# Hybrid decoder layer on one core: the sums of the second SwiGLU's down weights made by accumulating transfers that GpSimd issues, in place of adds on VectorE

## The chip, the core and the metric

One core of one Trainium2 chip runs the whole layer as one program. The core has a matrix engine (TensorE, PE in the profile), a vector engine (VectorE, DVE), an activation engine (ScalarE, ACT), a general engine (GpSimd, POOL), a queue processor that issues transfers (SyncE, SP), and 16 DMA engines that move data between HBM and the on-chip SBUF. The engines run side by side and each takes its instructions strictly in order; semaphores hold an instruction until what it needs is there. The metric is the time of the program on the device, in microseconds (us). A change of under 0.5% is about what a measurement of this kernel can't tell from none.

## The reference

The layer has three residual parts: a SwiGLU with half weight, a mixer with two kinds of attention, and a second SwiGLU with half weight.

```
h = swiglu(rms_norm(x, ff1_norm_pre), ...);   x = x + 0.5 * rms_norm(h, ff1_norm_post)
h = hybrid_mixer(rms_norm(x, mix_norm_pre));  x = x + rms_norm(h, mix_norm_post)
h = swiglu(rms_norm(x, ff2_norm_pre), ...);   x = x + 0.5 * rms_norm(h, ff2_norm_post)

def swiglu(h, w_gate, w_up, w_down):
    return (jax.nn.silu(h @ w_gate) * (h @ w_up)) @ w_down
```

There are 512 tokens of width 1024; the inner width of a SwiGLU is 2816. All is float32. The change concerns the last product of the second SwiGLU, `(...) @ w_down`.

## The kernel before, in words

**Precision.** A float32 product is made of three passes of TensorE: each operand is split into a high part (a copy rounded to the engine's fast format) and a low part (what is left), and high x high, high x low and low x high are added. A split costs one copy on ScalarE (sometimes on VectorE) for the high part and one subtraction on VectorE for the low part (`split`, lines 397 and 400 of the profile).

**Fewer products.** In the SwiGLUs a product of 2 x 2 blocks is made of seven block products instead of eight; for that some operands are sums of blocks. In the second SwiGLU's down product, 16 of the 22 row blocks of `w_down` go this way (`down_products`, `factor`, `down_product`), the other six, called plain pieces, the ordinary way (`down_piece`, `down_mm`). The seven products come in the order 1, 5, 6, 2, 7, 4, 3, with half of the first two plain pieces between 7 and 4. Each product takes its weights in four quarters q = 0 to 3, and each quarter is 12 matmuls of 512 columns. The tiles `ff2dw{m}{q}h` and `l` hold the high and low part of product m, quarter q.

**The sums.** With blocks B00, B01, B10 and B11 of the down weights, product 5 needs B00 + B01, product 6 that sum + B11, product 4 that + B10, and product 7 needs B01 + B11. Products 1, 2 and 3 take a block as it is. A running sum per quarter stands in the tile `ff2du{q}`. In the kernel before, every block comes from HBM into a tile `rawff2d...` by a transfer of 512 KB that SyncE issues (function `raw`, line 326 of the profile), and VectorE adds it (function `add`, line 594): four quarters for each of the products 5, 6, 7 and 4, so 16 adds.

**What sets the order.** All steps are written down as a graph (`Graph.op`), each with its engine, an estimated cost and the tiles it touches. `Graph.order` simulates the engines with those costs and lets each take, among the ready steps, the one with the highest level (longest way to the end, plus a number from the table `BIAS` for its kind). The result is a fixed list, and the program is emitted in that list's order. Tiles are slots of pools: 4 for `raw` tiles, 6 of kind `M` (the `ff2du` tiles stand there), 12 of kind `ring` (the split weights, two a quarter); a step waits until a slot is free.

**Around it.** Before the down products, the gate and up products (`product`, line 657) run, at the head of the program behind a norm: `n1{t}_xn` is the normed row block t, `n1{t}_t` its transpose on TensorE, and `xa1`, `xa2`, `xa4`, `xa8` the split transposes (two row blocks in each); `ff1q00w0` and the like are split gate (`ff1q00`) and up (`ff1q01`) weights.

Of the kernel before, what the change touches and what calls it, by code (L numbers as in the profile page):

```python
# [18 lines left out]
P = 128  # L19
# [34 lines left out]
    "ACT:fh>fdl": 2, "ACT:fh>fdl@ACT": -102.8, "ACT:fh>fhh": 18.2, "ACT:fh>fhh@DVE": -182, "ACT:fhr>fhh": -133.1,
    "ACT:fhr>fhh@ACT": -164.3, "ACT:fhr>fhh@DVE": 0.1, "ACT:fp_>fp_": 142.4, "ACT:fqu>fqw": 85.2,
    "ACT:fqv>fqw": 175.9, "ACT:fy>fdp": -30.4, "ACT:fy>o_ss": 22, "ACT:gr>gh": 1551.9, "ACT:htv>hTv": -9.6,
    "ACT:k__t>kT": 13.9, "ACT:ls>ls": 43.9, "ACT:n_nm>n_l": -61.2, "ACT:n_t>n_th": -21.2, "ACT:n_t>xa": -27.9,
    "ACT:n_t>xaf0": -166.3, "ACT:n_t>xc": 937.3, "ACT:n_t>xcf0": -5.8, "ACT:n_t>xcf1": -136.4,
# [9 lines left out]
    "ACT:xrv>Xv@ACT": 109.7, "ACT:z>o_ss": 7, "DVE:acc>oN": -12.4, "DVE:cd_t>kc": 14.2, "DVE:ck>kcT": -14.4,
    "DVE:cmask>cmb": -123.5, "DVE:cmask>gates": -28.4, "DVE:cmk>uk": -45.7, "DVE:cmv>uv": 35.2, "DVE:cv>vc": -35.9,
    "DVE:d>d_p": -19.3, "DVE:d_acc>o": 29.2, "DVE:d_r>d_p": 28.8, "DVE:d_t>d_th": 53.2, "DVE:dkt>dk": 5,  # L70
    "DVE:dl>d_r": -27.9, "DVE:dl>do_r": 19.2, "DVE:dmask>dmb": 14.2, "DVE:do_rr>o": 39.5, "DVE:do_t>oTd": -11,
    "DVE:fa>fh": 68.2, "DVE:fa>fhs": 89.7, "DVE:fb>fhs": -62.8, "DVE:fb>fp_": -55.6, "DVE:fc>fp_": -201.2,
    "DVE:fc__sg>fh": 23.8, "DVE:fd>fhs": 83.8, "DVE:fdp>fy": -4, "DVE:fdq>fy": 2.1, "DVE:fdr>fy": 3.8,
    "DVE:fh>fds": -7.5, "DVE:fh>fhl": 155.6, "DVE:fh>fhl@DVE": 9.3, "DVE:fh>fhl@POOL": 1.1, "DVE:fhr>fhl": 41.3,
    "DVE:fp_>fh": 50.6, "DVE:fp_>fp_": 4.3, "DVE:fqu>fqw": -345.7, "DVE:fqv>fqw": 43.8, "DVE:gates>nc_pc": 247,
    "DVE:gr>gh": 533.4, "DVE:gsub>gsub": 93.5, "DVE:htk>hTk": -0.9, "DVE:htv>hTv": 40.2, "DVE:k__t>kT": 53.3,
    "DVE:lamt>lp": -116.6, "DVE:lp>ls": 76.6, "DVE:n_cf>n_p@ACT": -63.4, "DVE:n_cf>n_p@DVE": -25.6,
# [9 lines left out]
    "DVE:xcf1>xcf1": -33, "DVE:xi>n_xn": 1575.3, "DVE:xj>n_xn": 161.1, "DVE:xm>n_xn": 62.1, "DVE:xrk>Xk@DVE": 51.4,  # L87
    "DVE:xrk>Xk@POOL": -0.9, "DVE:xrv>Xv": 53.6, "DVE:xrv>Xv@DVE": 124.3, "DVE:xrv>Xv@POOL": -18.4,
    "DVE:z>o_yg": 28.8, "PE:cd>kc": 18.3, "PE:d_p>o": 12.8, "PE:d_th>d_acc": -4, "PE:dkd>dk": -89.8,
    "PE:fqw>fa": -1.5, "PE:fqw>fb": 32.4, "PE:fqw>fc": 7923.9, "PE:fqw>fd": 39.8, "PE:gh>g_": 1645.8,  # L90
    "PE:k__dup>kT": -44, "PE:n_p>n_th": 266.8, "PE:n_th>acc": 854.1, "PE:n_xn>n_t": 60.2, "PE:n_xn>xb": -54.9,
# [1453 lines left out]
```

## Time and profile before

| | |
|---|---|
| time, median of 3 runs | 1007.09 us (1005.99 to 1009.65) |
| time of the profiled execution | 1006.28 us |
| its span, first to last instruction | 1004.5 us |
| TensorE busy | 991.2 us (99%) |
| VectorE busy | 831.7 us (83%) |
| ScalarE busy | 581.3 us (58%) |
| GpSimd busy | 34.5 us (3%) |
| read from HBM, written to HBM | 135.45 MB, 19.92 MB |

The profiled execution's time is 1.78 us over its span; that part lies outside the first and the last instruction. TensorE's busy time is modelled at the ends of its matmuls, so that a matmul that waits for its operand can still count as busy for a part of the wait; a wait shows best where the next start comes late. The granted TensorE clock averages 0.998 over the span.

### The profile page before, as it was taken

How to read it: one execution, taken by the hardware profiler on the slowest of the kernel's cores; microseconds unless marked ns; L12 is line 12 of the kernel's file. 1: busy time of each engine (PE TensorE's matmuls, PEld its weight loads, DVE VectorE, ACT ScalarE, POOL GpSimd, SP SyncE). 2: the span in 40 equal slices, each digit the busy share in tenths (PEclk: the TensorE clock that was granted, in tenths of full speed). 3: DMA queues.
4: the chain of work that ended last, by engine and by line, in shares of the span. 5: the costliest groups of instructions: out<-in, count | busy, mean ns of one | idle time of the engine just before them, and what ended most of it. 6: DMA issues, size and time to landing. Idle time of an engine off the chain costs nothing. (4 is left out here: it accounts for less than half of the span.)

```text
span 1004.5 us, 17263 instructions
## 1 busy us (share of the span) xinstructions
PE 991.2 (99%) x6552; PEld 901.5 (90%) x6552; DVE 831.7 (83%) x1564; ACT 581.3 (58%) x1141; POOL 34.5 (3%) x68
## 2 busy tenths in 40 slices
PE   8999999999999999999999999999999999999997
PEld 7999999999888889888888888899999999987776
DVE  7999989987565488578787799899989988999984
ACT  8645545555455365677777677776455554544442
POOL 1000000000000030000000001310000000000001
PEclk9999999999999999999999999999999999999999
DMA  9226514118999535840403052261335231386752
GB/s 319 80 86 177 178 43 156 56 43 279 367 354 370 186 122 186 324 168 1 168 1 141 28 191 87 81 230 64 128 104 168 70 101 43 105 278 225 237 203 84
DMA packets 98437, 156.49 MB, mean 156 GB/s; under 512 B 11185, under 2 KB 63665, under 8 KB 98354
## 3 DMA queue, kind: packets, MB, share of 16 engines
q1 hardware_dynamic: 98354, 155.40, 45.0%
q8 instruction: 51, 0.84, 0.3%
q14 instruction: 32, 0.26, 0.1%
HBM read 135.45 MB, written 19.92 MB: 155 GB/s over the span
## 5 line engine op out<-in xcount | busy, mean ns | idle before, releaser
L1195 ACT ACTIVATE n_p<-n_p,n_nm 128x128 f32<-128x128 f32 (+3 forms) x64 | 35.4, 556 | 9.3 <-DVE n_nm L1193 8.9
L346 DVE TENSOR_TENSOR pre<-pre 128x1024 fp32r<-128x1024 f32 x20 | 24.1, 1222 | 19.8 <-ACT pre L345 19.7
L345 ACT CAST pre<-pre 128x1024 fp32r<-128x1024 f32 x20 | 21.0, 1052 | 23.6 <-DMA pre<-w_in 14.4
L1193 DVE CUSTOM_DVE_ANT_0 n_p<-n,dmb 128x128 f32<-128x128 f32 (+3 forms) x64 | 28.3, 486 | 6.2 <-PE n L1183 5.8
L400 DVE TENSOR_TENSOR n_th<-n_t,n_th 128x512 fp32r<-128x512 f32 x40 | 25.8, 682 | 9.2 <-ACT n_th L397 9.1
L432 POOL TENSOR_SCALAR o_ms<-o_ss 128x1 f32<-128x1 f32 x12 | 4.2, 349 | 670.2 <-ACT junk L440 670.1
L397 ACT CAST n_th<-n_t 128x512 fp32r<-128x512 f32 x40 | 21.5, 594 | 9.7 <-PE n_t L1298 9.5
L684 ACT ACTIVATE ff2p<-ff2p 128x256 f32<-128x256 f32 x30 | 12.5, 417 | 17.2 <-DVE ff2p L696 17.1
L684 ACT ACTIVATE ff1p<-ff1p 128x256 f32<-128x256 f32 x30 | 12.5, 416 | 16.1 <-DVE ff1p L696 15.5
L696 DVE TENSOR_TENSOR ff1p<-ff1p,ff1b 128x512 f32<-128x512 f32 x30 | 20.3, 678 | 1.1 <-PE ff1b L657 1.0
L1298 PE MATMUL n_t<-ident,n_p 128*128 128x128 f32 x160 | 20.7, 272 | 0.0
L1298 PEld LDWEIGHTS n_t<-ident,n_p 128*128 128x128 f32 x160 | 18.6, 140 | 2.2
L1195 ACT ACTIVATE d_p<-d_p,d_nm 128x128 f32<-128x128 f32 (+3 forms) x32 | 17.8, 556 | 4.8 <-DVE d_nm L1193 4.8
L696 DVE TENSOR_TENSOR ff2p<-ff2p,ff2b 128x512 f32<-128x512 f32 x30 | 20.4, 679 | 0.2 <-PE ff2b L657 0.2
L1182 PE MATMUL n<-kT,qTn 128*128 128x128 f32 (+3 forms) x64 | 20.3, 334 | 0.0
L1183 PE MATMUL n<-kT,qTn 128*128 128x128 f32 (+3 forms) x64 | 19.6, 321 | 0.0
L440 ACT ACTIVATE junk<-ff2y 128x512 bf16<-128x512 f32 x8 | 4.8, 597 | 22.9 <-PE ff2y L761 22.9
L562 DVE TENSOR_TENSOR o_yg<-ff2y,g_ff_norm_post 128x512 f32<-128x512 f32 x8 | 5.5, 688 | 14.3 <-ACT junk L440 14.3
L391 PE MATMUL acc<-n_th,v 128*64 128x512 f32 x40 | 16.1, 402 | 0.0
L1193 DVE CUSTOM_DVE_ANT_0 d_p<-d,dmb 128x128 f32<-128x128 f32 (+3 forms) x32 | 14.9, 485 | 1.4 <-PE d L1183 1.0
L392 PE MATMUL acc<-n_th,v 128*128 128x512 f32 x40 | 15.7, 392 | 0.0
L463 PE MATMUL n_t<-ident,n_xn 128*128 128x128 f32 x96 | 13.7, 293 | 1.4 <-DVE n_xn L456 1.3
(1743 smaller groups left out, 3477.9 us busy)
## 6 DMA issues: line engine op xcount, KB each, us to landing
rawff2d<-ff_w_down SPq DMA_DIRECT2D x36, 512.0 KB, 4.9
...
```

Source lines behind the costliest of these rows:

```text
L345: op("ACT", act(n, 0.04), lambda: A.copy(hi(), raw()), r=[(k, 0)], w=[(k, 1)])
L346: op("DVE", dve(n), lambda: V.tensor_sub(T[k][:, 0, :n], raw(), f32(hi())), r=[(k, 1)], w=[(k, 0)], port=True)
L391: nc.tensor.matmul(oh, vh, b(1), start=False, stop=False)
L397: (A.copy if h.done == "ACT" else V.tensor_copy)(hi(), src())
L400: V.tensor_sub(lo(), src(), f32(hi()))
L684: op("ACT", act(256), lambda: A.activation(T[sg][:, :256], T[sg][:, :256], AF.Silu), w=[sg])
L696: op("DVE", dve(512), lambda: fn(T[out], T[x], T[y]), r=[k for k in (x, y) if k != out], w=[out])
L1182: nc.tensor.matmul(T[b][:, :L], qt[:, 0, h, :], k()[:, :L], start=True, stop=False)
L1183: nc.tensor.matmul(T[b][:, :L], qt[:, 1, h, :], k()[:, :L], start=False, stop=True)
L1193: op("DVE", dve(L), lambda: V.tensor_tensor_reduce(T[p][:, :L], T[b][:, :L], T["dmb"][:, S - L:], -1.0, 3e38, ALU.add, ALU.min, T[nm][:, 0 ...
L1195: op("ACT", act(L, 0.22), lambda: A.activation(T[p][:, :L], T[p][:, :L], AF.Exp, bias=T[nm][:, 0:1], scale=-1.0, accum_out=T[l][:, col:col ...
L1298: nc.tensor.transpose(T[bt][:, h * P:(h + 1) * P], T[p[h]][:, kb * P:(kb + 1) * P], ident)
```

## The change

In the second SwiGLU the four blocks for product 5 (and the first block of product 7) are loaded by SyncE straight into the tile that will hold the sum. The second block of each sum is then brought by a transfer that GpSimd issues and that adds to what the tile holds (`accum_op=ALU.add`). The planner gets an engine name `DQ` for these steps, with a cost of 1.5 and a latency of 3.0. The table `BIAS` is replaced as a whole (one line of it is shown).

```diff
-    "ACT:acc>ol": -8.4, "ACT:cd_t>kc": -50.8, "ACT:ck>kcT": 109.5, "ACT:cmk>prek": -60.1, "ACT:cmv>prev": -32.4,
...
+    "ACT:acc>ol": -8.4, "ACT:ck>kcT": 109.5, "ACT:cmk>prek": -60.1, "ACT:cmv>prev": -16.6, "ACT:cv>vc": -36.7,
...
-    LAT = {"PE": 0.28, "ACT": 0.18, "DVE": 0.2, "POOL": 0.2, "SP": 2.0}
+    LAT = {"PE": 0.28, "ACT": 0.18, "DVE": 0.2, "POOL": 0.2, "SP": 2.0, "DQ": 3.0}
...
+        def src(q, kh, jh):
+            r0 = (2 * SPILL + 8 * kh + 2 * q) * P
+            return io[f"{f}_w_down"][0, r0:r0 + 2 * P, jh * 512:(jh + 1) * 512].rearrange("(k p) b -> p k b", p=P)
+
         def raw(q, kh, jh, tag):
-            k, r0 = new(f"raw{f}d{tag}{q}{kh}{jh}", "raw", [P, 1024]), (2 * SPILL + 8 * kh + 2 * q) * P
-            v = lambda: T[k].rearrange("p (a b) -> p a b", a=2)
-            pdma.append(load(k, v, io[f"{f}_w_down"][0, r0:r0 + 2 * P, jh * 512:(jh + 1) * 512].rearrange("(k p) b -> p k b", p=P), chain="dma"))
+            k = tag if isinstance(tag, str) else new(f"raw{f}d{tag}{q}{kh}{jh}", "raw", [P, 1024])
+            pdma.append(load(k, lambda: T[k].rearrange("p (a b) -> p a b", a=2), src(q, kh, jh), chain="dma"))
             return k
 
-        def add(dst, a, b, r):
-            op("DVE", dve(1024), lambda: V.tensor_add(T[dst], T[a], T[b]), r=[k for k in r if k != dst], w=[dst], port=True, chain="sum")
+        def add(dst, q, kh, jh):
+
+            op("DQ", 1.5, lambda: nc.gpsimd.dma_start(T[dst].rearrange("p (a b) -> p a b", a=2), src(q, kh, jh), accum_op=ALU.add),
+               w=[dst], chain="sum")
...
             if m == 5:
-                a, b = raw(q, 0, 0, m), raw(q, 0, 1, m)
-                add(u, a, b, [a, b])
+                raw(q, 0, 0, u)
+                add(u, q, 0, 1)
             elif m == 6:
-                b = raw(q, 1, 1, m)
-                add(u, u, b, [b])
+                add(u, q, 1, 1)
             elif m == 4:
-                b = raw(q, 1, 0, m)
-                add(u, u, b, [b])
+                add(u, q, 1, 0)
             elif m == 7:
-                u, b = raw(q, 0, 1, m), raw(q, 1, 1, m)
-                add(u, u, b, [b])
+                u = raw(q, 0, 1, m)
+                add(u, q, 1, 1)
```

The order of TensorE's instructions is the same in both programs, row by row. VectorE's moves in the first tenth and in the last quarter of the program, ScalarE's in a few places there too.

VectorE where the weights of products 5 and 6 are split (`ff2dw5..`, `ff2dw6..`; the rows `ff2dl..` and `ff2ds` belong to the other operand), before:

```order
L400 TENSOR_TENSOR ff2dw52l_10841<-ff2du2_10817,ff2dw52h_10834 128x1024
L594 TENSOR_TENSOR ff2du3_10859<-rawff2d5300_10796,rawff2d5301_10813 128x1024
L594 TENSOR_TENSOR ff2du0_10748<-ff2du0_10748,rawff2d6011_10836 128x1024
L594 TENSOR_TENSOR ff2du1_10777<-ff2du1_10777,rawff2d6111_10839 128x1024
L400 TENSOR_TENSOR ff2dw53l_10887<-ff2du3_10859,ff2dw53h_10866 128x1024
L400 TENSOR_TENSOR ff2dw60l_10893<-ff2du0_10748,ff2dw60h_10883 128x1024
L400 TENSOR_TENSOR ff2dw61l_10909<-ff2du1_10777,ff2dw61h_10889 128x1024
```

And the same place in the changed program:

```order
L401 TENSOR_TENSOR ff2dw52l_10827<-ff2du2_10638,ff2dw52h_10748 128x1024
L401 TENSOR_TENSOR ff2dl51_10791<-ff2ds_10602,ff2dl51_10791 128x1024
L401 TENSOR_TENSOR ff2dw53l_10832<-ff2du3_10669,ff2dw53h_10783 128x1024
L401 TENSOR_TENSOR ff2dl60_10825<-ff2ds_10602,ff2dl60_10825 128x1024
L778 TENSOR_TENSOR ff2ds_10602<-ff2ds_10602,ff2h1_9479 128x1024
L401 TENSOR_TENSOR ff2dw60l_10869<-ff2du0_10604,ff2dw60h_10847 128x1024
L401 TENSOR_TENSOR ff2dw61l_10875<-ff2du1_10621,ff2dw61h_10851 128x1024
```

The adds (line 594) are gone from VectorE, and the splits and sums of the other operand have moved up between the weight splits.

GpSimd at the same stage in the changed program, where it had no instruction before (its neighbours before and after stood next to each other):

```order
L434 TENSOR_TENSOR n33_r_8045<-n33_ms_8046,mhalf_73 128x1
L599 DMA ff2du0_10604<-ff2_w_down 128x2x512
L599 DMA ff2du1_10621<-ff2_w_down 128x2x512
L599 DMA ff2du2_10638<-ff2_w_down 128x2x512
L599 DMA ff2du3_10669<-ff2_w_down 128x2x512
L599 DMA ff2du0_10604<-ff2_w_down 128x2x512
L599 DMA ff2du1_10621<-ff2_w_down 128x2x512
L599 DMA ff2du2_10638<-ff2_w_down 128x2x512
L599 DMA ff2du3_10669<-ff2_w_down 128x2x512
L599 DMA rawff2d7001_10951<-ff2_w_down 128x2x512
```

The first four bring B01 for product 5, the next four B11 for product 6; the row shown last and three more for product 7 and four for product 4 follow, and then the last norms.

VectorE at the head of the program, from the split of the second row block on, before:

```order
L400 TENSOR_TENSOR xa1_279<-n11_t0_302,xa1_279 128x4x128
L400 TENSOR_TENSOR xa2_290<-n11_t1_308,xa2_290 128x4x128
L456 SCALAR_TENSOR_TENSOR n12_xn0_356<-xi2_272,n12_r_345,g1_0_236 128x512
L538 TENSOR_TENSOR ff1q01w0_349<-rawff1q010_294,ff1q01w0_349 128x512
L538 TENSOR_TENSOR ff1q01w2_358<-rawff1q011_313,ff1q01w2_358 128x512
L538 TENSOR_TENSOR ff1q00w1_361<-rawff1q000_244,ff1q00w1_361 128x512
L538 TENSOR_TENSOR ff1q00w2_354<-rawff1q001_258,ff1q00w2_354 128x512
L538 TENSOR_TENSOR ff1q01w1_371<-rawff1q010_294,ff1q01w1_371 128x512
```

And in the changed program:

```order
L401 TENSOR_TENSOR xa1_279<-n11_t0_302,xa1_279 128x4x128
L539 TENSOR_TENSOR ff1q01w0_344<-rawff1q010_294,ff1q01w0_344 128x512
L457 SCALAR_TENSOR_TENSOR n12_xn0_358<-xi2_272,n12_r_346,g1_0_236 128x512
L539 TENSOR_TENSOR ff1q00w2_350<-rawff1q001_258,ff1q00w2_350 128x512
L539 TENSOR_TENSOR ff1q01w2_356<-rawff1q011_313,ff1q01w2_356 128x512
L539 TENSOR_TENSOR ff1q00w1_372<-rawff1q000_244,ff1q00w1_372 128x512
L539 TENSOR_TENSOR ff1q01w1_377<-rawff1q010_294,ff1q01w1_377 128x512
L401 TENSOR_TENSOR xa2_290<-n11_t1_308,xa2_290 128x4x128
```

The split of `xa2` has moved from before the norm `n12_xn0` to behind four weight splits.

## Rows read from the trace of the kernel before

**Rows 1.** The page: busy us of each engine, share of the span, instructions.
```profile
PE 991.2 (99%) x6552; PEld 901.5 (90%) x6552; DVE 831.7 (83%) x1564; ACT 581.3 (58%) x1141; POOL 34.5 (3%) x68
```

**Rows 2.** Windows of the down stage: us, busy by engine, clock, DMA share, GB/s.
```profile
870.00:885.00 15.00, 15.00 (x128) 15.00 (x127) 13.79 (x18) 6.41 (x9) 0.00 (x0) 1.00 0.50 166
885.00:910.00 25.00, 25.00 (x113) 20.61 (x112) 22.66 (x22) 12.44 (x13) 0.00 (x0) 1.00 0.84 287
910.00:930.00 20.00, 19.13 (x84) 15.50 (x83) 18.23 (x20) 9.96 (x11) 0.00 (x0) 1.00 0.67 223
930.00:950.00 20.00, 19.12 (x83) 15.00 (x82) 19.29 (x20) 7.92 (x9) 0.00 (x0) 1.00 0.78 262
950.00:972.00 22.00, 21.54 (x95) 17.16 (x93) 22.00 (x26) 14.20 (x16) 0.00 (x0) 1.00 0.73 264
```

**Rows 3.** Chain that ended last, down stage: start us, us, what.
```profile
885.39 24.58 PE ff2y L801 x108
...
971.95 26.18 PE ff2y L761 x114
998.17 0.04 issue
```

**Rows 4.** Waits of TensorE, 880 to 1000 us: us in total, times, longest.
```profile
PE ff2y L801 <- DVE ff2dl L400: 1.2, 2, 0.9
PE ff2y L801 <- DVE ff2dw73l L400: 0.8, 1, 0.8
```

**Rows 5.** Groups of instructions: the adds; busy us, mean ns, idle before them.
```profile
L594 DVE TENSOR_TENSOR ff2du<-ff2du,rawff2d 128x1024 f32<-128x1024 f32 x8 | 9.7, 1221 | 2.0 <-DMA rawff2d<-ff_w_down 1.9
...
L594 DVE TENSOR_TENSOR rawff2d<-rawff2d,rawff2d 128x1024 f32<-128x1024 f32 x4 | 4.9, 1221 | 2.0 <-DMA rawff2d<-ff_w_down 2.0
L594 DVE TENSOR_TENSOR ff2du<-rawff2d,rawff2d 128x1024 f32<-128x1024 f32 x4 | 4.9, 1217 | 0.7 <-DMA rawff2d<-ff_w_down 0.7
```

**Rows 6.** The tile rawff2d: its loads, issue ns; us from issue to landing.
```profile
L326 SPq DMA_DIRECT2D rawff2d<-ff_w_down x36: 367/368/470, 854.8 to 951.7; - x36
...
DMA to landing us min/median/max: 3.5/4.9/6.9
```

**Rows 7.** Timeline of SyncE, 850 to 872 us: product 1's four loads.
```profile
854.75 16.47 SPq L326 DMA_DIRECT2D rawff2d<-ff_w_down  x4
```

**Rows 8.** Timeline of TensorE: its first matmul with product 6's last quarter.
```profile
915.23 0.39 PE L801 MATMUL ff2y<-ff2dw63h,ff2dl 128*128 128x512 f32 x1
```

**Rows 9.** TensorE's matmuls with product 4's last quarter, first and last start.
```profile
L801 PE MATMUL ff2y<-ff2dw43h,ff2dl x8: 389/389/389, 956.1 to 958.6; 128*128 128x512 f32 x8
```

**Rows 10.** Timeline of ScalarE, the high part of one quarter.
```profile
899.28 1.05 ACT L397 CAST ff2dw53h<-ff2du 128x1024 fp32r<-128x1024 f32 x1 [0.25 <-DVE ff2du L594]
```

**Rows 11.** Timeline of VectorE, the low part of the same quarter.
```profile
903.19 1.22 DVE L400 TENSOR_TENSOR ff2dw53l<-ff2du,ff2dw53h 128x1024 fp32r<-128x1024 f32 x1
```

**Rows 12.** Timeline of VectorE at the head of the program.
```profile
14.63 0.69 DVE L400 TENSOR_TENSOR xa<-n_t,xa 128x512 fp32r<-128x512 f32 x1 [1.08 <-ACT xa L397]
15.24 0.74 DVE L456 SCALAR_TENSOR_TENSOR n_xn<-xi,n_r,g 128x512 f32<-128x512 f32 x1
15.90 1.28 DVE L538 TENSOR_TENSOR ff1q01w<-rawff1q,ff1q01w 128x512 fp32r<-128x512 f32 x2
17.10 1.28 DVE L538 TENSOR_TENSOR ff1q00w<-rawff1q,ff1q00w 128x512 fp32r<-128x512 f32 x2
...
28.55 1.28 DVE L400 TENSOR_TENSOR xa<-n_t,xa 128x512 fp32r<-128x512 f32 x2
```

**Rows 13.** Timeline of GpSimd at the head: the third norm's factor.
```profile
14.61 0.56 POOL L433 TENSOR_TENSOR n_r<-n_ms,mhalf 128x1 f32<-128x1 f32 x1
```

**Rows 14.** Timeline of TensorE at the head.
```profile
13.61 1.58 PE L657 MATMUL ff1a<-xa,ff1q00w 128*128 128x256 f32 x11 [0.72 <-DVE xa L400]
16.13 0.63 PE L463 MATMUL n_t<-ident,n_xn 128*128 128x128 f32 x4 [0.93 <-DVE n_xn L456]
...
18.03 1.88 PE L657 MATMUL ff1a<-xa,ff1q00w 128*128 128x256 f32 x12
...
29.29 1.57 PE L657 MATMUL ff1c<-xa,ff1q00w 128*128 128x256 f32 x11 [0.69 <-DVE xa L400]
```

More of the change, by code (lines that the diff above doesn't have):

```diff
@@ L54 @@
[L54 to L58, printed above, removed]
@@ L68 @@
[L68 to L72, printed above, removed]
@@ L73 @@
[L73 to L77, printed above, removed]
@@ L87 @@
[L87 to L91, printed above, removed]
@@ new lines @@
+    "ACT:fdu>fdwh": -72.2, "ACT:fdu>fdwh@DVE": 28.9, "ACT:fh>fdl": 2, "ACT:fh>fdl@ACT": -102.8,
+    "ACT:fh>fdl@DVE": -2.1, "ACT:fh>fhh": 20.1, "ACT:fh>fhh@ACT": -24.5, "ACT:fh>fhh@DVE": -182,
+    "ACT:fhr>fhh": -133.1, "ACT:fhr>fhh@DVE": 0.1, "ACT:fp_>fp_": 142.4, "ACT:fqu>fqw": 48.1, "ACT:fqv>fqw": 318.7,
+    "ACT:fy>fdp": -26.3, "ACT:fy>o_ss": 25.2, "ACT:gr>gh": 1796.4, "ACT:htv>hTv": 11.3, "ACT:k__t>kT": 13.9,
+    "ACT:ls>ls": 43.9, "ACT:n_nm>n_l": -63.2, "ACT:n_t>n_th": -51.6, "ACT:n_t>xa": -27.9, "ACT:n_t>xaf0": -166.3,
@@ new lines @@
+    "ACT:xcf1>xc@DVE": -52.3, "ACT:xm>n_ss": 98.5, "ACT:xrk>Xk": -40.3, "ACT:xrk>Xk@ACT": -10.8,
+    "ACT:xrk>Xk@DVE": 135.5, "ACT:xrv>Xv": 175.3, "ACT:xrv>Xv@ACT": 109.7, "ACT:z>o_ss": 25.5, "DQ:fdu>fdu": -11.7,
+    "DVE:acc>oN": -14.1, "DVE:cd_t>kc": 14.2, "DVE:cmask>cmb": -122.1, "DVE:cmask>gates": -28.4, "DVE:cmk>uk": -45.7,
+    "DVE:cmv>uv": 28, "DVE:cv>vc": -35.9, "DVE:d>d_p": -19.3, "DVE:d_acc>o": 29.2, "DVE:d_r>d_p": 28.8,
+    "DVE:d_t>d_th": 53.2, "DVE:dkt>dk": 5, "DVE:dl>d_r": -27.9, "DVE:dl>do_r": 19.2, "DVE:dmask>dmb": 14.2,
@@ new lines @@
+    "DVE:do_rr>o": 39.5, "DVE:do_t>oTd": -11, "DVE:fa>fh": 74.6, "DVE:fa>fhs": 89.7, "DVE:fb>fhs": -72.9,
+    "DVE:fb>fp_": 1.2, "DVE:fc>fhs": -4.3, "DVE:fc>fp_": -201.2, "DVE:fc__sg>fh": 23.8, "DVE:fd>fhs": 83.8,
+    "DVE:fdp>fy": -2.4, "DVE:fdq>fy": 2.1, "DVE:fdr>fy": 3.8, "DVE:fh>fds": -7.5, "DVE:fh>fhl": 155.6,
+    "DVE:fh>fhl@DVE": 9.3, "DVE:fh>fhl@POOL": 1.1, "DVE:fhr>fhl": 41.3, "DVE:fp_>fh": 199.2, "DVE:fp_>fp_": 5,
+    "DVE:fqu>fqw": -122.6, "DVE:fqv>fqw": 47.9, "DVE:fy>fdr": 6.4, "DVE:gates>nc_pc": 247, "DVE:gr>gh": 753.5,
@@ new lines @@
+    "PE:wp>uv": 27.9, "PE:wp>z": 19.1, "PE:wv>cv": -122, "POOL:Xv>Xv": 7.5, "POOL:do_r>do_rr": -36.3,
+    "POOL:do_ss>do_r": 8.7, "POOL:n_ss>n_r": 550.7, "POOL:o_ss>o_r": -5.6, "SP:cmask>cmask": 143.6,
+    "SP:fhd>fhr": 87.3, "SP:g_ff1_norm_post>g_ff1_norm_post": 7, "SP:g_ff2_norm_post>g_ff2_norm_post": -1,
+    "SP:g_ff2_norm_pre>g_ff2_norm_pre": 91.2, "SP:g_mix_norm_post>g_mix_norm_post": 2.8,
+    "SP:g_mix_norm_pre>g_mix_norm_pre": -47.1, "SP:gr>gr": 1061.8, "SP:low>wp": 241.5, "SP:pev>pev": -17.8,
@@ L104 @@
+    "SP:pre>low": 193, "SP:pre>pre": -164.5, "SP:raw>raw": -1796.8, "SP:rawff1q>rawff1q": 1456.4,
+    "SP:rawff2d>rawff2d": 1.6, "SP:rawff2q>rawff2q": 178, "SP:trig>trig": 12.3, "SP:wrk>wrk": 4.8, "SP:wrv>wrv": 77.7,
+    "SP:x>xo": 2.7, "SP:xi>xi": 93.1, "SP:xj>x": 15.3, "SP:xj>xj": -15.6, "SP:xm>x": -28.2, "SP:xm>xm": -3.5,
+    "SP:xo>xo": -14.6,
 }
@@ L239, in order @@
                             for p in self.tiles[k][0]:
-                                heapq.heappush(back, (o.end + self.LAT[e] * (e != "SP"), p, k))
+                                heapq.heappush(back, (o.end + self.LAT[e] * (e not in ("SP", "DQ")), p, k))
                     for y, data in o.outs:
-                        lat = 0.0 if y.eng == (e,) and e != "SP" else self.LAT[e]
+                        lat = 0.0 if y.eng == (e,) and e not in ("SP", "DQ") else self.LAT[e]
                         y.at = max(y.at, o.end + lat if data else o.start + 1e-6)
```

47 lines of the change are left out of this document (22 added, 25 removed), and 16 rows, old and new, of the table BIAS.

## The prediction

> **What bounds the kernel now.** I read the page's engine totals first: TensorE is busy 991.2 us of the span of 1004.5, VectorE 831.7, GpSimd 34.5 [rows 1]. TensorE bounds the program, so VectorE's 16 adds count only by the time for which TensorE stands still for them. The windows of the down stage come next [rows 2]: the granted clock is 1.00 throughout, so nothing is to be had from the clock, and VectorE is busy 13.79 + 22.66 + 18.23 + 19.29 + 22.00 = 95.97 us of the 102 from 870 to 972, of the 87 from 885 on 82.2 (94%). GpSimd does nothing there, and the DMA engines are at 0.50 to 0.84. The chain of waits runs through TensorE's matmuls from 885.39 to 998.17 without another engine in between [rows 3]. So the down products take 998.17 - 885.39 = 112.78 us, and the question is how much of it is standing still.
>
> Two readings give it. The stage has 7 products of 4 x 12 matmuls and 6 plain pieces of 24, 336 + 144 = 480 matmuls. At the pace of the first stretch, 24.58 / 108 = 0.2276 us each, they need 109.25 us, which leaves 3.5 us. That is an upper bound, since the tail may have a slower pace of its own. The windows show 0.87 + 0.88 + 0.46 = 2.2 us without a matmul in 910 to 972 [rows 2], a lower bound, since a waiting matmul counts as busy for part of its wait. The list of waits names VectorE's splits `ff2dl` (1.2 us) and `ff2dw73l` (0.8 us) [rows 4]: VectorE is what ends last here, and it is in turn held by adds which wait for loads, 1.9 + 2.0 + 0.7 = 4.6 us of idle time ahead of them, mostly put down to a DMA [rows 5].
>
> **The change part by part.**
>
> *The adds go.* 16 adds cost VectorE 9.7 + 4.9 + 4.9 = 19.5 us [rows 5]. VectorE then has 82.2 - 19.5 = 62.7 us of work in 87 (72%); even with a few casts moved to it from ScalarE, at most 3 x 1.2 = 3.7 us by the add of the same shape, it stays under 77%. With a quarter of its time free it no longer makes TensorE wait, if its inputs come. The gain is between 2.2 and 3.5 us; I take 3.0, nearer to the upper reading, since the lower leaves out the part of a wait that counts as busy. It can't be 19.5 us: TensorE does not stand still that long.
>
> *SyncE issues fewer loads.* 36 issues become 20; 16 x 0.37 = 5.9 us less of queue time [rows 6]. No engine waits for SyncE's own time here, so this is worth nothing by itself.
>
> *GpSimd's accumulates.* Sixteen transfers of 0.524 MB take over the second read of each sum. GpSimd is free (0.00 busy in all five windows [rows 2]), so issuing costs no one else. What counts is when they land. The first can start when the tile's first block is there: SyncE's queue has product 1's four loads until 854.75 + 16.47 = 871.2 [rows 7], and the loads behind them land a median of 4.9 us after issue [rows 6], so about 876.1 (an estimate from these two rows). Product 6's last quarter is first used at 915.23 [rows 8], and needs before that a cast of 1.05 [rows 10], a subtraction of 1.22 [rows 11] and about 0.1 of handing over, 2.4 us; so the eighth accumulate must have landed by 912.8. If GpSimd's transfers go one after another, each may take (912.8 - 876.1) / 8 = 4.6 us. The sixteenth, for product 4's last quarter, first used at 956.1 [rows 9], must be in by 956.1 - 1.8 (the waits of before ahead of it, gone) - 2.4 = 951.9: 75.8 / 16 = 4.7 us each. If several are in flight together, as SyncE's loads are, only the latency of one counts, and 8 us would do.
> No row shows a transfer from GpSimd, nor one that adds to what it finds. The nearest rows are SyncE's loads of the same block, at 3.5, 4.9 and 6.9 us from issue to landing [rows 6]. One after another at 3.5 us the accumulates are early by 20 us (3.0 gained); at 4.9 they end 16 x 4.9 = 78.4 after the start, 2.6 us late; at 6.9, 110.4, 34.6 us late. In flight together all three prices are in time. I take them as in flight together: the transfers are independent within a group of four, wait for different tiles, and SyncE's loads overlap (a landing of 4.9 us against an issue of 0.37). Cost 0, with the serial cases kept for the range.
>
> The Trainium skill ("DMA: Bandwidth & Descriptors", section "Anatomy of one DMA — SWDGE (gpsimd) path") gives a transfer from GpSimd 2.0 us plus its bytes at 436 GB/s: 3.2 us for one of these, an estimate, eight in a row 25.6, in by 901.7; by it the sum stays 3.0 us gained. Against the change speaks "Collectives: The Full Stack", section "The bandwidth ceiling: the fold count and why AG ≠ RS ≠ AR": a transfer that reduces reads two sources and runs at half the rate of a copy. Put together that is 2.0 + 2.4 = 4.4 us, eight in a row in by 911.3, so still in time but barely. No row here shows either.
>
> *The order at the head.* The new table also reorders VectorE where the program starts. The split `xa2` of the second row block stood before the norm `n12_xn0`; now it stands behind it and four weight splits. `n12_xn0` began at 15.24 [rows 12], and can't come much earlier, because the norm's factor is ready at 14.61 + 0.56 = 15.17 [rows 13]. So `xa2` now ends near 15.24 + 0.66 + 4 x 0.60 (starts at 15.90 and 17.10 for two each) + 0.69 = 18.99. TensorE began the matmuls with it at 18.03 and took 1.88 us for 12; the other groups show 1.57 to 1.58 for 11 [rows 14], about 1.6 without a hole, so it was effectively free to run from 18.3. That is +0.7 us. At 29.29 there was a wait of 0.69 for the split from 28.55 [rows 12, 14]; one weight split (0.60) now stands ahead of it, so 28.55 + 0.60 + 0.69 = 29.84, +0.6. The two don't fully add, since a TensorE that is late at 18 needs the later one later: +0.7 for both, between -0.5 (some of the waits there, 0.72 + 0.93 + 0.69 = 2.3, fall away) and +1.3 (both). TensorE's order is the same in both programs, so what is lost at the head isn't caught up.
>
> *The tail* behind 998.17 is the same work in the same order: 0.
>
> **Sum.** 1006.28 (the profiled execution) - 3.0 + 0.7 = 1004.0 us. The median of the runs, 1007.09, is 0.81 above the profiled one, which belongs in the range rather than in the sum.
>
> **The rivals.**
>
> *Accumulates one after another, and slower than 4.7 us each (slower).* Place: GpSimd's transfer queue during the down products. For it: an accumulate has to read its target as well, one queue feeds all, and the landing times of plain loads reach 6.9 us with the DMA engines at 0.84. Against it: SyncE's loads overlap. The adds' wait moves to TensorE, and each product is late by what the queue lacks: 16y - 75.8. At y = 4.9, 2.6 us: 1004.0 + 2.6 = 1006.6; at 5.9, 18.6 us: 1022.6; at 6.9, 34.6 us: 1038.6. The point of decision is 4.7 us. Chance 0.20.
>
> *The accumulates overlap but load the DMA engines twice.* In 885 to 972 these are busy 0.84 x 25 + 0.67 x 20 + 0.78 x 20 + 0.73 x 22 = 66.1 us and move 287 x 25 + 223 x 20 + 262 x 20 + 264 x 22 kB = 22.7 MB, 2.91 us a MB, 1.53 us per block. If an accumulate takes twice that, 16 x 1.53 = 24.4 us come on top, against 20.9 free there and 15 x 0.50 = 7.5 ahead: it just fits, loads land later and about half of the gain is lost, 1005.5. At three times it would be 48.9, 20 more than fits, about 1024. Chance 0.08.
>
> *More is gained.* The free VectorE takes all 3.5 us away, and the head gains 0.5: 1006.28 - 3.5 - 0.5 = 1002.3; with the head's other waits gone too (2.3 in place of 0.5) 1000.5. For it: TensorE is not busy for 1004.5 - 991.2 = 13.3 us of the span [rows 1], of which the places above hold 2.2 + 2.3 = 4.5, and the new table moves a few instructions at others. Against it: the order changes little outside the head and the down stage, the factor's time at 15.17 holds the head, and a reordering can lose as well. Chance 0.20.
>
> **How the numbers follow.** Forecast 0.52, own range 1002 to 1006; rival one 0.20, rival two 0.08, more gained 0.20. A measurement can't tell less than 0.5% from none, 5.04 us of 1007.09: faster is below 1002.05, slower above 1012.1. Below 1002.05 I put a tenth of the forecast (0.05) and three quarters of "more gained" (0.15), 0.20 with rounding up to 0.21 for what the spread between profiled execution and median adds. Above 1012.1 lie three quarters of rival one (0.15) and a third of rival two (0.03): 0.18. Between them 0.61. The range of 1001 to 1012.5 leaves out a quarter of "more gained" (0.05) and most of the serial cases (0.15).
>
> **What would show it.** Right: TensorE's windows from 910 to 972 full, VectorE near 63 us of busy time in 885 to 972, no wait for `ff2dw5` to `ff2dw7` splits, GpSimd's transfers in flight two or more at a time and landed 2.4 us before use; at the head, TensorE's block of 18.03 beginning near 19, that of 29.29 near 29.8. Wrong: splits or casts of `ff2dw6` and `ff2dw4` idle behind a DMA, landings evenly spaced at more than 4.7 us (rival one); landings of SyncE's loads well above 4.9 us and a DMA share near 1 (rival two); a head that starts its blocks as early as before (more gained).

## The result and the profile after

The changed kernel takes 1057.24 us (median, 1055.36 to 1060.14), the kernel before 1006.65 beside it: a ratio of 1.0504, with a 95% interval of 1.0483 to 1.0525. Forecast were 1004.0 us, with a range of 1001 to 1012.5. The first rival, GpSimd's transfers one after another, is what happened, and further out than its worst price of 1038.6.

The page's totals of the changed kernel come first, to be held against [rows 1], and its row of granted clock in 40 slices:

```profile
PE 1006.2 (95%) x6552; PEld 910.0 (86%) x6552; DVE 815.0 (77%) x1549; ACT 579.0 (55%) x1140; POOL 53.8 (5%) x84
...
PEclk9999999999999999999999999999999999688799
```

VectorE has 831.7 - 815.0 = 16.7 us less to do, as the change promises. TensorE, with the same 6552 matmuls, shows 15 us more, and the clock is below full speed in four of the last six slices. The windows say where (columns as in [rows 2]; the stretch before 885 is left out, one behind 972 is added):

```profile
885.00:910.00 25.00, 12.45 (x60) 10.17 (x59) 3.44 (x5) 3.46 (x4) 3.67 (x3) 0.79 0.74 183
910.00:930.00 20.00, 15.20 (x56) 12.37 (x57) 12.29 (x12) 6.32 (x8) 3.65 (x3) 0.75 0.33 56
930.00:950.00 20.00, 12.00 (x40) 8.89 (x40) 10.44 (x10) 7.77 (x8) 1.22 (x1) 0.74 0.38 76
950.00:972.00 22.00, 18.76 (x73) 14.34 (x71) 8.52 (x9) 3.98 (x4) 3.65 (x3) 0.92 0.70 162
972.00:1010.00 38.00, 27.76 (x90) 19.97 (x89) 21.09 (x23) 13.10 (x15) 6.09 (x5) 0.82 0.82 210
```

Every window from 885 on is short of matmuls: 12.45 of 25, 15.20 of 20, 12.00 of 20. VectorE is down to 3.44 us in the window in which it had 22.66 before: it waits too. The list of TensorE's waits, 880 to 1012 us (us in all, times, longest), is headed, in place of the 2.0 us of [rows 4], by:

```profile
PE ff2y L805 <- DVE ff2dw50l L401: 17.4, 1, 17.4
PE ff2y L805 <- ACT ff2dl L398: 9.8, 2, 8.0
PE ff2y L805 <- DVE ff2dr L812: 3.8, 1, 3.8
PE ff2y L765 <- ACT ff2hh L398: 2.8, 1, 2.8
```

The whole difference is in this stage. Between the first and the last matmul of the down products lie 997.73 - 885.23 = 112.5 us before and 1049.84 - 886.15 = 163.7 after, 51.2 more, and the two spans differ by 1056.7 - 1004.5 = 52.2. The distances between neighbouring starts of these matmuls split it. Those of 0.5 us and more, beyond the normal 0.2276, hold 43.9 us after (18 of them) and 2.9 before; those between 0.28 and 0.5 us hold 10.9 us (58) and 0.6. The first are stalls, +41 us. The second are matmuls at the lower clock behind stalls, +10 us, which the timeline of TensorE (start us, us, what, idle before it) shows behind the longest one:

```profile
897.06 0.39 PE L805 MATMUL ff2y<-ff2dw50h,ff2dl 128*128 128x512 f32 x1
914.80 0.79 PE L805 MATMUL ff2y<-ff2dw50l,ff2dl 128*128 128x512 f32 x1 [17.35 <-DVE ff2dw50l L401]
...
917.95 1.05 PE L805 MATMUL ff2y<-ff2dw50h,ff2dl 128*128 128x512 f32 x2
...
920.28 0.62 PE L805 MATMUL ff2y<-ff2dw51h,ff2dl 128*128 128x512 f32 x2
```

A pair takes 1.05 us at 917.95 and 0.62 at 920.28: from 914.80 on twelve matmuls start 0.43 us apart, after that 0.23 as before. After 17 us with nothing to do TensorE ran for 5 us at about half its speed: the granted clock is 0.50 from 914.8 to 919.6, the lower of its two levels (1.2 and 2.4 GHz), and 1.00 from 920.1 to 924.

The view that explains the stalls is GpSimd's timeline (start us, us, what, idle before it, and what ended the idle time):

```profile
877.75 1.39 POOL L599 DMA_DIRECT2D ff2du<-ff_w_down  x1 [212.25 <-DVE ff2dw10l L401]
887.70 1.23 POOL L599 DMA_DIRECT2D ff2du<-ff_w_down  x1 [8.56 <-issue]
897.58 1.21 POOL L599 DMA_DIRECT2D ff2du<-ff_w_down  x1 [8.64 <-issue]
904.74 1.23 POOL L599 DMA_DIRECT2D ff2du<-ff_w_down  x1 [5.95 <-issue]
915.40 1.21 POOL L599 DMA_DIRECT2D ff2du<-ff_w_down  x1 [9.44 <-DVE ff2dw50l L401]
...
927.66 1.21 POOL L599 DMA_DIRECT2D ff2du<-ff_w_down  x1 [4.86 <-issue]
933.69 1.22 POOL L599 DMA_DIRECT2D ff2du<-ff_w_down  x1 [4.82 <-issue]
951.23 1.21 POOL L599 DMA_DIRECT2D rawff2d<-ff_w_down  x1 [16.31 <-DVE ff2dw22l L401]
...
1000.88 1.22 POOL L599 DMA_DIRECT2D ff2du<-ff_w_down  x1 [6.89 <-issue]
```

An accumulate occupies GpSimd for 1.2 us, and then the next one doesn't start until the one before it has landed (the first lands at 887.43, the second starts at 887.70): "issue" is put down for 5 to 9 us, though the first four go to four different tiles, all loaded by 882. They begin 6.0 to 6.2 us apart where little else is moved, 9.9 us where SyncE's loads run beside them. The sixteenth begins at 1000.88; by the prediction it had to be in by 951.9.

### The profile page after: what moved, and what is told of

Read it like the earlier page. It is cut to its first block, busy times and chain, and to the rows that moved or that the text cites. A ratio compares the mean times of both kernels' runs of the same rounds, so it can differ in the third digit from the quotient of the medians.

```text
span 1056.7 us, 17260 instructions
## 1 busy us (share of the span) xinstructions
PE 1006.2 (95%) x6552; PEld 910.0 (86%) x6552; DVE 815.0 (77%) x1549; ACT 579.0 (55%) x1140; POOL 53.8 (5%) x84
## 3 DMA queue, kind: packets, MB, share of 16 engines
q0 software_dynamic: 4352, 8.39, 4.8%
## 5 line engine op out<-in xcount | busy, mean ns | idle before, releaser
L599 POOL DMA_DIRECT2D ff2du<-ff_w_down x12 | 14.8, 1234 | 282.0 <-DVE ff2dw10l L401 212.3
L689 DVE TENSOR_TENSOR ff2h<-ff2p 128x256 f32<-128x256 f32 x24 | 10.1, 419 | 23.6 <-ACT ff2p L688 23.6
L805 PE MATMUL ff2y<-ff2dw50l,ff2dl 128*128 128x512 f32 x4 | 2.7, 670 | 17.4 <-DVE ff2dw50l L401 17.4
```

## Experiments

**The table of numbers alone.** The first experiment keeps the new table and gives the sums back to VectorE, and the second blocks to SyncE:

```diff
-            op("DQ", 1.5, lambda: nc.gpsimd.dma_start(..., src(q, kh, jh), accum_op=ALU.add), w=[dst], chain="sum")
+            op("DVE", dve(1024), lambda: V.tensor_add(T[dst], T[a], T[b]), ..., w=[dst], port=True, chain="sum")
```

Expected: 

> The changed program with its table of numbers, but the sums made by VectorE from loads that SyncE issues, as before the change. It tells the table (and the head that it reorders) from the accumulating transfers. Theory A (the 52 us come from the accumulates alone): 1004 to 1008 us, ratio to before 0.997 to 1.002, no wait of TensorE over 1.5 us behind 880 us. Rival (the table's order costs a part): 1010 us or more, with waits that stand in the trace of the changed kernel too.

Measured: 1008.19 us, ratio 1.0013 (1.0002 to 1.0025). The new table costs 0.1%, at most 0.25%; the accumulates cost the other 5%. At the head the wait for `xa2` is there as foretold, 1.66 us, and the block that began at 29.29 [rows 14] begins at 29.60. Ahead of the prediction it was said that TensorE's order is the same in both programs; at the head that isn't so. Before, four transposes (16.13, [rows 14]) stood ahead of twelve matmuls of the first block; with the new table the twelve stand ahead of them:

```profile
14.56 1.92 PE L664 MATMUL ff1a<-xa,ff1q01w 128*128 128x256 f32 x12
16.32 0.60 PE L464 MATMUL n_t<-ident,n_xn 128*128 128x128 f32 x4
...
18.69 1.58 PE L664 MATMUL ff1a<-xa,ff1q00w 128*128 128x256 f32 x11 [1.66 <-DVE xa L401]
...
29.60 1.57 PE L664 MATMUL ff1c<-xa,ff1q00w 128*128 128x256 f32 x11 [0.63 <-DVE xa L401]
```

**Space for descriptors.** The program sets aside 1024 bytes of SBUF per partition for the descriptors of GpSimd's transfers. The second experiment is the changed kernel, with the same order on all engines, and

```diff
-    nc = bacc.Bacc(..., dynamic_dma_scratch_size=1024)
+    nc = bacc.Bacc(..., dynamic_dma_scratch_size=2048)
```

Expected: 

> The changed program, instruction for instruction in the same order, with 2048 in place of 1024 bytes of SBUF per partition set aside for the descriptors of GpSimd's transfers. Theory A (the space holds the descriptors of one accumulate only, so the next can't be issued until it has landed): the four accumulates for product 5 go out within 4 to 6 us of each other's tiles being ready, the fourth lands by about 895 in place of 910.2 us, and most of the first two stalls (17.4 and 8.0 us) goes: 1012 to 1035 us. Theory B (GpSimd's queue or the DMA engines take one accumulate at a time whatever the space): the starts stay 6.0 to 9.9 us apart, 1054 to 1060 us.

Measured: 1025.13 us, ratio 1.0187 (1.0173 to 1.0201). One number takes 32 of the 50 us away. GpSimd's timeline:

```profile
878.79 1.39 POOL L599 DMA_DIRECT2D ff2du<-ff_w_down  x1 [212.13 <-DVE ff2dw10l L401]
880.41 2.49 POOL L599 DMA_DIRECT2D ff2du<-ff_w_down  x2 [0.22 <-DMA ff2du<-ff_w_down]
887.78 1.23 POOL L599 DMA_DIRECT2D ff2du<-ff_w_down  x1 [4.88 <-DMA ff2du<-ff_w_down]
```

Now three go out within 4 us (878.79, 880.41 and the second of the x2), and the fourth waits until the first has landed (887.51): the space held one accumulate and now holds three. Theory A stands, theory B has fallen. The fourth lands at 899.9 in place of 910.6.

**A plain transfer from GpSimd.** Kernel of the first experiment, with the 16 second blocks loaded by `nc.gpsimd.dma_start(...)` without `accum_op`, and added by VectorE.

```diff
-            pdma.append(load(k, ..., src(q, kh, jh), chain="dma"))
+            op("DQ", 1.5, lambda: nc.gpsimd.dma_start(T[k]..., src(q, kh, jh)), w=[k], chain="dma")
```

Expected: 

> The kernel of the first run, with the 16 second blocks loaded by GpSimd in place of SyncE, plainly, and added by VectorE. It tells the queue from the adding. Theory B1 (whatever GpSimd issues goes one at a time): starts at least 5 us apart also when tiles are free, 1020 to 1050 us. Theory B2 (only a transfer that adds goes one at a time): several in flight, landings in 5 to 8 us, 1004 to 1012 us. Theory A (space for descriptors): between, since a plain transfer may need less space than one that reads its target too: two or more in flight, 1004 to 1020 us.

Measured: 1012.69 us, ratio 1.0060 (1.0046 to 1.0073). With the same 1024 bytes up to three are in flight: when the two of 898.35, below, have gone out, the load of 893.04 has not landed. They take 0.72 us to issue instead of 1.22 and land in 5.4 us (median):

```profile
898.35 1.44 POOL L599 DMA_DIRECT2D rawff2d<-ff_w_down  x2 [4.57 <-DVE ff2du L603]
902.89 0.72 POOL L599 DMA_DIRECT2D rawff2d<-ff_w_down  x1 [3.10 <-DVE ff2du L603]
```

So it isn't a rule that GpSimd's transfers go one at a time. Most of their idle time here ends with a tile becoming free. The 4.5 us that this kernel is above the first one stand mostly at the matmuls of `ff2dw62`, which wait for splits of the other operand, `ff2dl` (2.4 and 1.2 us). ScalarE has the first of these splits' casts, at 915.76, behind `ff2dw63h`, whose sum waits for a load issued at 904.12 and landed at 911.55: again a step that stands behind one that waits.

**Halves.** Each accumulate of the changed kernel cut into two of 256 KB, space 1024.

```diff
-            nc.gpsimd.dma_start(T[dst].rearrange(...), src(q, kh, jh), accum_op=ALU.add)
+            for a in range(2):
+                nc.gpsimd.dma_start(T[dst].rearrange(...)[:, a], src(q, kh, jh)[:, a], accum_op=ALU.add)
```

Expected: 

> The changed program with each accumulate cut into two of 256 KB, one row block each, in the same places of the order. Theory A (space): two halves fit where one whole did, so the second is issued while the first moves; a pair takes 5 to 6.5 us where nothing else loads the DMA engines, and the time is 1045 to 1062 us. Theory B (one transfer at a time): each half pays the fixed part of about 2.4 us (issue to first packet 1.9 and 0.3 to 0.5 behind the last) again, a pair takes 8 to 8.5 us instead of 6.1, 16 x 2.2 = 35 us more in the queue, 1070 to 1095 us.

Measured: 1031.33 us, ratio 1.0244 (1.0230 to 1.0258), better than either theory said. Three halves go out at once, then one for each that lands:

```profile
877.61 2.88 POOL L601 DMA_DIRECT2D ff2du<-ff_w_down  x3 [212.15 <-DVE ff2dw10l L401]
884.50 0.90 POOL L601 DMA_DIRECT2D ff2du<-ff_w_down  x1 [4.00 <-issue]
```

The space holds three halves where it held one whole, so half an accumulate more moves at a time, and the fixed part of each is hidden. It is the second, independent sign of the same limit. The tenth and the twelfth run, below, agree: with 2048 bytes seven halves are in flight, and the eighth goes out when the first has landed.

**The planner told the truth.** Only the planner's cost of an accumulate is changed:

```diff
-    LAT = {..., "DQ": 3.0}      op("DQ", 1.5, ...)
+    LAT = {..., "DQ": 0.3}      op("DQ", 6.1, ...)
```

Expected: 

> The changed program with one number pair changed: the planner is told 6.1 us and 0.3 us of latency for an accumulate (what the trace shows for one alone) instead of 1.5 and 3.0. The space stays 1024, the order of TensorE stays, ScalarE and VectorE take their steps behind 870 us in another order. Theory A1 (two causes: one accumulate at a time, and on ScalarE and VectorE casts that wait for an accumulate stand ahead of steps that wait for nothing, as ff2dw52h and ff2dw53h ahead of the last ff2p, so that the low part of ff2dw50 starts 26 us after its accumulate landed): the first stall falls from 17.4 to about 8 us, and the later accumulates start earlier: 1030 to 1045 us. Rival A2 (the queue of accumulates alone decides): 1050 to 1058 us.

Measured: 1047.55 us, ratio 1.0410 (1.0392 to 1.0429): 9.7 us are gone without any transfer being faster. That lies between the two ranges: A1 is right in kind, but the queue decides more than it said. What was wrong in the order is seen in the changed kernel on ScalarE and VectorE (timelines):

```profile
887.51 1.05 ACT L398 CAST ff2dw50h<-ff2du 128x1024 fp32r<-128x1024 f32 x1 [6.54 <-DMA ff2du<-ff_w_down]
...
904.51 1.04 ACT L398 CAST ff2dw52h<-ff2du 128x1024 fp32r<-128x1024 f32 x1 [6.05 <-DMA ff2du<-ff_w_down]
...
910.66 1.04 ACT L398 CAST ff2dw53h<-ff2du 128x1024 fp32r<-128x1024 f32 x1 [4.79 <-DMA ff2du<-ff_w_down]
911.61 0.41 ACT L688 ACTIVATE ff2p<-ff2p 128x256 f32<-128x256 f32 x1
```
```profile
885.06 1.22 DVE L401 TENSOR_TENSOR ff2dw13l<-rawff2d,ff2dw13h 128x1024 fp32r<-128x1024 f32 x1
905.90 0.43 DVE L689 TENSOR_TENSOR ff2h<-ff2p 128x256 f32<-128x256 f32 x1 [19.62 <-ACT ff2p L688]
...
912.05 0.42 DVE L689 TENSOR_TENSOR ff2h<-ff2p 128x256 f32<-128x256 f32 x1 [3.99 <-ACT ff2p L688]
...
913.53 1.22 DVE L401 TENSOR_TENSOR ff2dw50l<-ff2du,ff2dw50h 128x1024 fp32r<-128x1024 f32 x1
```

The accumulate for `ff2dw50` was in by 887.5, and its cast ran at once. Its low part (`ff2dw50l`, line 401) began at 913.53. It stands on VectorE behind `ff2h` (905.90 and 912.05), which needs `ff2p` from ScalarE (line 688), which stands there behind the casts `ff2dw52h` and `ff2dw53h`, which wait for the third and the fourth accumulate. So a step for the first weights waited for the last transfer of its group, over two engines. In the retold order the first stall of 17.4 us is gone; what stands in its place are waits of at most 2.4 us.

**Both.** Space 2048, and the planner told 3.5 and 6.0 us.

```diff
+    nc = bacc.Bacc(..., dynamic_dma_scratch_size=2048)
+    LAT = {..., "DQ": 6.0}      op("DQ", 3.5, ...)
```

Expected: 

> The changed program with both: 2048 bytes of space, and the planner told 3.5 us and 6.0 us of latency. Theory A1: both causes are eased, 1008 to 1018 us, with no stall of the first weights ff2dw50. Rival A2 (the space alone): as with 2048 bytes before, 1023 to 1027 us.

Measured: 1014.96 us, ratio 1.0082 (1.0067 to 1.0098). Alone they gave 32.1 and 9.7 us, together 42.3: two causes that add, as near as this can show, since the planner was told other numbers here than alone. Of the waits of TensorE one is left that counts:

```profile
PE ff2y L805 <- ACT ff2dw73h L398: 4.5, 1, 4.5
```

**Accumulates only where there is time.** The kernel before with its own table, space 1024, the planner told 6.1 and 0.3; accumulates (the step `acc`) for product 7 only, and then for product 4 only.

```diff
             elif m == 7:
-                u, b = raw(q, 0, 1, m), raw(q, 1, 1, m)
-                add(u, u, b, [b])
+                u = raw(q, 0, 1, m)
+                acc(u, q, 1, 1)
```
```diff
             elif m == 4:
-                b = raw(q, 1, 0, m)
-                add(u, u, b, [b])
+                acc(u, q, 1, 0)
```

Expected: 

> The kernel before with its own table; only the four adds for product 7 become accumulates, with the space of 1024 and the planner told 6.1 and 0.3 us. Four accumulates of 6 us have some 40 us to land in. Theory A (only lateness costs): no stall at ff2dw70 to ff2dw73, the 0.8 us wait for ff2dw73l goes, 1004 to 1007 us, ratio 0.997 to 1.001. Rival C (an accumulate costs by its presence, since it takes the DMA engines twice the time for its bytes and so delays SyncE's loads): 1009 us or more with waits for loads of the other products.

Measured: 1019.45 us, ratio 1.0126 (1.0112 to 1.0139). Theory A was off, and rival C's range holds without its reason, since TensorE waits for product 7's own weights: product 7 has no slack. Its accumulates go into a `raw` tile whose own load comes first, and with 4 such tiles that load waits for product 2's to be split. GpSimd starts them at 919.11, 927.36, 933.41 and 939.52; TensorE is at product 7 from 929.2 on and waits 2.6 to 4.9 us for each of the other quarters. With adds the two loads run side by side; an accumulate puts them in a row. That is only a part of it: the four tiles are loaded by 924.2, and the last three accumulates still start 0.3 us after the one before has landed (927.09, 933.14, 939.20), the queue of one again. In the eleventh run, with 2048 bytes, the four have landed by 939.0 instead of 945.8. How the 12.8 us divide no run shows.

Expected: 

> The same with the four adds for product 4 alone. Theory A: the accumulates have from product 6's splits to product 4, some 35 us, and land in time: 1004 to 1007 us, ratio 0.997 to 1.001. Rival C: 1009 us or more.

Measured: 1009.83 us, ratio 1.0031 (1.0020 to 1.0041). All four land by 937, no split of product 4 is waited for, and still it is slower by 3 us: rival C, an accumulate costs by its presence. Its windows row, against DMA 0.67 and TensorE 19.13 in [rows 2], and VectorE's timeline:

```profile
910.00:930.00 20.00, 17.12 (x75) 13.54 (x74) 16.12 (x17) 7.95 (x9) 2.45 (x2) 1.00 0.95 260
```
```profile
917.14 1.23 DVE L400 TENSOR_TENSOR ff2dw22l<-rawff2d,ff2dw22h 128x1024 fp32r<-128x1024 f32 x1 [1.20 <-ACT ff2dw22h L397]
919.70 1.23 DVE L400 TENSOR_TENSOR ff2dw23l<-rawff2d,ff2dw23h 128x1024 fp32r<-128x1024 f32 x1 [1.34 <-ACT ff2dw23h L397]
```

Before, the four splits of product 2 ran without a gap (`ff2dw22l` at 915.68, `ff2dw23l` at 916.81); here these two wait for their casts, and the casts for SyncE's loads. VectorE's order is the same as before until 942, ScalarE's until 946, and SyncE's issues come at the same times: the load for `ff2dw22h` went out at 907.84 before and landed in 3.6 us; here it goes out at 908.02, beside an accumulate, and takes 7.9. Behind these splits on VectorE comes `ff2dl`, for which TensorE waits 2.4 us (0.9 before). SyncE's loads issued from 900 to 930 took 6.6 us to land in the mean, 4.8 before. The DMA queues of the changed kernel, 870 to 1010 us (packets, MB, share of 16 engines), show why:

```profile
q0 software_dynamic: 4352, 8.39, 36.3%
q1 hardware_dynamic: 6336, 14.68, 30.3%
```

36.3% of 140 us for 8.39 MB are 6.1 us of all engines' time a MB; SyncE's plain transfers need 30.3% for 14.68 MB, 2.9 us a MB. An accumulate takes the DMA engines 2.1 times as long as a load.

**Half the bytes, and halves with 2048.** Both on the kernel with space 2048 and the planner told; the second with the diff of the halves above.

```diff
-            nc.gpsimd.dma_start(T[dst].rearrange(...), src(q, kh, jh), accum_op=ALU.add)
+            nc.gpsimd.dma_start(T[dst].rearrange(...)[:, 0], src(q, kh, jh)[:, 0], accum_op=ALU.add)
```

Expected: 

> The kernel of the sixth run (space 2048, the planner told 3.5 and 6.0 us), with the same 16 accumulates in the same places, but each brings only the first of its two row blocks, 256 KB; the second half of every sum is left out, so half of the added blocks is missing from the output. It tells what is left over before the change, about 8 us, apart. Theory D (the DMA engines: an accumulate's packet takes 178 ns against 84 of a plain one, three at once hold up each other and SyncE's loads): landings of 5 to 6.5 us in place of 8 to 12, 1005 to 1009 us. Rival E (the accumulate has to wait for its target's load, so two landings stand in a row before every cast; the order of VectorE and ScalarE): little change, 1012 to 1015 us.

Measured: 1011.02 us, ratio 1.0030 (1.0018 to 1.0043), between the two.

Expected: 

> The kernel of the sixth run with each accumulate cut into two of 256 KB, all bytes moved. Theory D (the DMA engines' time is what is left over): the bytes are the same, so no gain beyond a quicker first half: 1011 to 1017 us. Rival F (still the space for descriptors, and the latency of a whole one): 1005 to 1010 us.

Measured: 1014.17 us, ratio 1.0053 (1.0035 to 1.0072), within theory D's range; this doesn't tell it from E. With half the bytes the accumulates for product 7 had landed by 930.0, yet TensorE stood for 3.0 us until 942.3, for the same `ff2dw73h`. So it wasn't its own accumulate that this cast waited for. ScalarE's timeline in the sixth run:

```profile
943.23 1.04 ACT L398 CAST wp63h<-raw 128x1024 fp32r<-128x1024 f32 x1 [4.52 <-DMA raw<-ff_w_down]
944.18 1.04 ACT L398 CAST ff2dw73h<-rawff2d 128x1024 fp32r<-128x1024 f32 x1
```

The cast that TensorE needs, with its input in since 939.3, stands behind that of a plain piece, whose load is late: it goes out at 935.21 (935.13 before), but beside the accumulates it takes 8.0 us to land, not 4.6. So theories D and E each have a part in this stall: the accumulates make that load late, and the order hands the lateness on to a cast that doesn't need it.

**One cast moved.** The sixth run, with the plain pieces' casts made to follow `ff2dw73h`:

```diff
-        plain = {c: down_piece(f, c) for c in range(EARLY)}
+        plain = {c: down_piece(f, c, g.writers[f"{f}dw73h"]) for c in range(EARLY)}
```

Expected: 

> The kernel of the sixth run (whole accumulates, space 2048, the planner told 3.5 and 6.0 us) with one step of ScalarE moved: the cast ff2dw73h, which stood behind the casts of the plain pieces wp62 and wp63, goes ahead of them. Half the bytes (the ninth run) had not removed the stall at ff2dw73h: its accumulate had landed at 929.6 and TensorE waited until 942.3. Theory E (order: the cast stands behind wp63h, whose load is late): the stall of 4.5 us goes and the time falls by 4 to 6 us, 1008 to 1012 us. Theory D (the DMA engines' time): no change beyond 1 us, 1013 to 1016 us, the stall comes back elsewhere.

Measured: 1007.69 us, ratio 1.0014 (1.0001 to 1.0027): 7 us for one step's place (the planner also moved the cast `ff2dw72h` from VectorE to ScalarE and swapped two steps on VectorE). That is slightly more than theory E asked for, since the matmuls at the lower clock behind the stall go with it (granted 0.54 from 944 to 950 in the sixth run, 1.00 here). And the same edit on the halves:

Expected: 

> The kernel of the tenth run (halves, space 2048) with the same step moved. Theory E: the stall of 3.5 us at ff2dw73h goes, 1008 to 1011 us, at best level with before. Theory D: 1012 to 1015 us. In neither is it faster than before by more than 0.3%, since the 3 us that VectorE's adds cost there are all that is to be had.

Measured: 1008.73 us, ratio 1.0014 (1.0005 to 1.0023), so 4 to 5 us (by the ratios or by the medians). Both stand where the first experiment stands, the new table with VectorE's adds (1.0013). With the queue, the order and the place of the cast put right, the accumulates neither gain nor lose. No version beat the kernel before. Why nothing is gained shows in the waits of TensorE in the eleventh run, and in two of its windows:

```profile
PE ff2y L805 <- DVE ff2dw63l L401: 1.1, 1, 1.1
PE ff2y L805 <- DVE ff2dw43l L401: 0.8, 1, 0.8
PE ff2y L805 <- DVE ff2dw70l L401: 0.6, 1, 0.6
PE ff2y L805 <- DVE ff2dw73l L401: 0.4, 1, 0.4
```
```profile
885.00:910.00 25.00, 25.00 (x116) 20.88 (x116) 17.33 (x18) 9.72 (x12) 6.07 (x5) 1.00 1.10 263
910.00:930.00 20.00, 18.88 (x83) 15.04 (x82) 18.77 (x18) 10.15 (x11) 3.80 (x3) 1.00 0.60 149
930.00:950.00 20.00, 18.95 (x82) 14.57 (x81) 14.93 (x17) 10.47 (x11) 6.10 (x5) 1.00 1.09 245
950.00:972.00 22.00, 21.24 (x93) 17.13 (x92) 15.18 (x18) 9.98 (x12) 0.00 (x0) 1.00 0.86 297
```

2.9 us of waits for splits, 2.0 before. VectorE has 17.33 + 18.77 + 14.93 + 15.18 = 66.2 us of work in 87, a quarter of its time free. The splits are late because their inputs land late: all four are of accumulated weights, the accumulates take 6.4 to 14.9 us to land, and the DMA share is 1.10 and 1.09 in two of the windows, where it was 0.84 and 0.78.

## Why the prediction was wrong

*The accumulates, "cost 0".* This is the step that failed: of the two ways in which sixteen transfers can go, I took "in flight together", because SyncE's loads go so. They went one after another, 6.0 to 10 us from start to start, with 1024 bytes for their descriptors. The experiment with 2048 shows the cause. The nearest row was of another engine's queue, and it spoke of the price of a transfer, not of how many fit. The line of the program that sets the space aside had been there to read.

*The price of the serial case.* Rival one had the mechanism and the place right, and at its worst nearly the price of a transfer: the sixteen are in flight for 108.5 us, 6.8 each, where its highest bound, from SyncE's landings, was 6.9; 0.3 us lie between a landing and the next start. What its sum left out is that the queue can stand empty: for 4.8 us before 915.40 and 11.7 before 951.23, when the next accumulate waited for splits that were late themselves (`ff2dw50l`, `ff2dw22l`). From 877.75 (876.1 foretold) to the last landing at 1006.9 that makes 108.5 + 13 x 0.3 + 16.5 = 129 us; less the 75.8 that there were, 53 us, against 51 measured. The rival got a chance of 0.20; nothing in the rows had excluded it.

*Moved steps.* The prediction counted three casts moved to VectorE and looked no further into the order of ScalarE and VectorE in this stage. There the planner's 1.5 us an accumulate had put casts that wait ahead of a step that waits for nothing. Worth 9.7 us: in the retold order the sixteen are in flight for 106.7 us, hardly less, but the queue stands empty only once, for 7.4 us in place of 16.5. A row of waits of before can't show it, only the order read beside a landing time can.

*The DMA engines.* Rival two named the doubled load, and the queue rows and the experiment with product 4 alone show it (2.1 times). Its price of 1.5 us for sixteen was too low: four of them cost 3 us, since product 2's loads land so close to their use that 4 us more for one of them reached TensorE.

*VectorE's adds, "2.2 to 3.5 us gained".* The adds are gone and VectorE has the time that I computed (66.2 of 87 us, "under 77%"). But even in the best version TensorE waits no less. That a free engine no longer makes others wait "if its inputs come" was stated, and the condition is what failed.

*The head, +0.7.* Right in kind: a wait of 1.66 us for `xa2` in the place foretold. `n_xn`'s wait of 0.93 is gone, since twelve matmuls now run ahead of the transposes, a change of TensorE's order that the prediction took to be absent. The size is +0.3 to +0.4 (29.29 to 29.60 in the first experiment, 29.70 in the changed kernel), as the bounds allowed. At the first matmul of the down products these two are 0.7 and 0.9 us late; where the rest arises was not followed.

Of the Trainium skill's two rules, a copy's fit of "DMA: Bandwidth & Descriptors" (section "Anatomy of one DMA — SWDGE (gpsimd) path") gave an estimate of 3.2 us a transfer; the rows show 6.1 from one accumulate to the next, and 5.4 (median; 4.0 at the least) for a plain load from GpSimd. The halved rate that "Collectives: The Full Stack" (section "The bandwidth ceiling: the fold count and why AG ≠ RS ≠ AR") gives for a reduce agrees with the 2.1 times here. Put together they came to an estimate of 4.4 us, 2.0 fixed and 2.4 of moving. In the trace 1.9 us lie between the start of the issue (1.2 of them GpSimd's own) and the first packet, 3.5 between the first and the last, and 0.6 from there to the next issue, so 2.5 fixed and 3.5 of moving: most of what is missing lies in the moving.

Left open: what plain loads from GpSimd would cost in an order made for them; and how much of the 3 us that the eleventh run doesn't gain is the doubled transfer time and how much the row of load and accumulate, since half the bytes were tried only with the cast in its old place.
